# Which engine forms the low parts of the weights, and a planner whose clocks know that DVE and POOL share a way into SBUF

## The chip, the cores and the metric

The kernel runs on one NeuronCore of a Trainium2 chip. The core has five engines with instruction queues of their own: PE (matrix multiplications), DVE (vector operations), ACT (functions and casts), POOL (vector operations on the GpSimd cores) and SP, which here only issues DMAs. Each engine works through its queue in order and waits at its head for what the instruction there needs. Time is device microseconds (us) of one execution. The number compared is the median of several runs.

## The reference

Two blocks follow each other on 256 tokens of width 1024, all in float32. The first block is one layer of a hybrid mixer (two attentions, a gated linear attention, a recurrent unit) and a mixture of 32 experts. The second block has two layers, and each layer is

```python
for i in range(2):
    f = swiglu(rmsnorm(h, ffn1_pre_g[i]), ffn1_w_gate[i], ffn1_w_up[i], ffn1_w_down[i])
    h = h + 0.5 * rmsnorm(f, ffn1_post_g[i])
    m = mixer(rmsnorm(h, mix_pre_g[i]), ...)      # SSD branch + S5 branch, gated, then w_out
    h = h + rmsnorm(m, mix_post_g[i])
    f = swiglu(rmsnorm(h, ffn2_pre_g[i]), ffn2_w_gate[i], ffn2_w_up[i], ffn2_w_down[i])
    h = h + 0.5 * rmsnorm(f, ffn2_post_g[i])
```

`swiglu` is `(silu(x @ w_gate) * (x @ w_up)) @ w_down` with a hidden width of 2816. The mixer multiplies by `w_in`, runs a state space model in chunks (SSD) on one branch and a diagonal complex recurrence (S5) on the other, and multiplies by `w_branch_a`, `w_glu`, `w_branch_b` and `w_out`.

## The kernel before

A product of two float32 matrices is made of three products of a shorter format, fp32r: each operand is split into a high part (the value rounded to fp32r) and a low part (the value less its high part), and PE forms high by high, high by low and low by high (`mm3`). All weights of the dense layers are split on the chip.

**How weights flow.** A unit of weights is 128x2048 floats, 1 MB. SP loads units one after the other into a ring of raw buffers (tiles named `..._raw`). Each unit has two halves of 128x1024. For each half, ACT casts the raw half to the high part (`split_high`, L368, tiles `..._whi`), and then DVE or POOL subtracts the high part from the raw half (`split_low`, L376, tiles `..._wlo`). The subtraction is called "a low" below. `low` (L359) chooses its engine. When both lows of a unit are formed, its raw buffer is free (`drop`) and SP may load the next unit into it. High and low parts live in rings of four halves in the second block, three raw buffers feed them, and PE spends 24 matmuls of 128x256 on each half.

**What sets the order.** The kernel is written out by a planner that runs when the program is built. Every instruction goes through `Engine` (L131), which keeps a clock for each engine: an instruction starts at the latest of its engine's clock and the times at which its operands are written or free, and it ends after a cost by formula (`on_vector`, `on_gpsimd` and so on). The clocks are those of an estimate; on the chip only the order on each queue is left of them. In the stages with `static = False` (the first mixer and the whole second block) the clocks decide three things. `pump` (L339) decides when a high part or a low is put in a queue. `low` decides which engine gets a low: before the change POOL has it if it ends there in time for PE (0.5 us before PE is due at that half, 2.57 us of PE for each half in front of it) or if POOL would end before DVE, and DVE has it otherwise. `either` (L552) chooses DVE or POOL for some other vector operations by their clocks, and `stir` (L466) lets the side work ("threads": the activations of a feed-forward layer, the SSD and S5 branches, the building of the S5 matrices) issue its next step when their clocks are not too far ahead of PE's. During the mixture of experts the order is fixed (`static`), and there `low` isn't asked in this way.

**The stages** of the profiled run, by their borders in us: first mixer with routing 0 to 278, experts 278 to 1255, and then, for each of the two layers of the second block, feed-forward 1, mixer, feed-forward 2: 1255 to 1512, 1512 to 1965, 1965 to 2206, 2206 to 2408, 2408 to 2859, 2859 to 3067. While the first and the third of these six run, `s5_build` (L1007) loads the tables of the S5 matrices of the mixer to come with many small DMAs (tiles `s5b_p`) and multiplies them on whichever engine `either` names.

Names in rows: the part before the first underscore is the stage or thread that made the tile (`ffn`, `bnd` for the boundary between layers, `u`, `z`, `x`, `g`, `glu`, `bb`, `ba`, `wo` for products of the mixer, `ssd`, `dt`, `s5i`, `s5o`, `s5b` for its side work, `k` for what lasts). Since every operation is recorded by `Engine`, all rows have one line, L155.

Of the kernel before, what the change touches and what calls it, by code (L numbers as in the profile page):

```python
# [29 lines left out]
class FM:  # L30


    def __init__(self, tiles):
        self.tiles = tiles
# [8 lines left out]
class Clocks:  # L43
# [4 lines left out]
    def __init__(self, nc):  # L48
        self.nc, self.times, self.base = nc, {}, {}
        self.dma = self.queue = self.end = 0.0  # L50
        self.count, self.table = 0, None
        self.vector, self.gpsimd = Engine(nc.vector, self.on_vector, self), Engine(nc.gpsimd, self.on_gpsimd, self)
        self.scalar, self.tensor, self.sync = Engine(nc.scalar, self.on_scalar, self), Engine(nc.tensor, self.on_tensor, self), Engine(nc.sync, None, self)

    def __getattr__(self, name):
        return getattr(self.nc, name)
# [49 lines left out]
    def busy(self, name):  # L106
        return max([max(t[:2]) for t in self.times.get(name, {}).values()], default=0.0)

    def on_vector(self, name, out, args, kw):
        n = max(a.free_size() for a in (out, *args) if isinstance(a, bass.AP))  # L110
        return 0.07 + 0.06 * any(isinstance(a, bass.AP) and a.free_size() == 1 for a in args) + n * (0.0063 if name == "reciprocal" else 0.00052 if name in self.SINGLE else 0.00104)
# [19 lines left out]
class Engine:  # L131
# [3 lines left out]
    def __getattr__(self, name):  # L135
        f, c = getattr(self.engine, name), self.clocks

        def call(out, *args, **kw):
            w = [out] + [kw[k] for k in ("accum_out",) if k in kw]
            r = [a for a in (*args, *kw.values()) if isinstance(a, bass.AP) and a is not kw.get("accum_out")]  # L140
            start = max([self.clock] + [c.written(a, self) for a in r] + [c.touched(a, self) for a in w])
            if name == "dma_start":
                self.clock = start + (1.0 if self is c.gpsimd else 0.1)
                c.queue = max(c.queue, start) + 0.45
                c.dma = max(c.dma, c.queue + 1.1) + self.spread(out, r)
                end = c.dma + 1.9
            else:
                end = self.clock = start + self.cost(name, out, args, kw)
            for a in w:
                c.mark(a, end, self)  # L150
            for a in r:
                c.mark(a, end)
            c.end = max(c.end, end)
            c.count += 1
            return f(out, *args, **kw)  # L155
        return call
# [22 lines left out]
class Core:  # L179
# [179 lines left out]
    def low(self, h):  # L359

        if self.static:
            return self.q if h % 4 == 3 and self.keys[self.order[h // 2]][0] in self.LENT else self.v
        c = self.nc
        hi = c.written(self.halves[h][0])
        pool = max(self.q.clock, hi) + 2.3
        return self.q if pool <= max(c.tensor.clock + (h - self.uh) * 2.57 - self.LEAN, max(self.v.clock, hi) + 1.14) else self.v

    def split_high(self):  # L368
        u, i = self.order[self.sh // 2], self.sh % 2
# [1262 lines left out]
class Kernel(Block2):  # L1632
# [590 lines left out]
    def mixer1(self, x):  # L2223
# [68 lines left out]
        for j, (n, _) in enumerate(self.WIN):  # L2292
# [9 lines left out]
            if n == "cqk":  # L2302
                def low():
                    nc.scalar.copy(gl, gps)
                    self.give(ps=1)
                self.defer(low)
# [690 lines left out]
```

## Time and profile before

| | |
|---|---|
| median of 3 runs | 3071.73 us (3071.64 to 3073.94) |
| profiled execution | 3076.65 us, its span 3074.4 us |
| PE busy | 2668.1 us, 87% |
| DVE busy | 1689.6 us, 55% |
| POOL busy | 1442.4 us, 47% |
| ACT busy | 1020.0 us, 33% |
| mean granted TensorE clock | 0.950 |

"Busy" of DVE and POOL counts an instruction from its start to its end as recorded, with any time in which it stood still inside it. [...] A "chain" is the work that ended last, followed back from the last instruction.

### The profile page before, as it was taken

To read this page: it belongs to the slowest core of one execution; us is meant where nothing else is said; L and a number is where in the kernel's file an instruction comes from. 1 tells how busy PE (TensorE), PEld (TensorE's weight loads), DVE (VectorE), ACT (ScalarE), POOL (GpSimd) and SP (SyncE) were. 2 spreads that over 40 slices of the span, in tenths; PEclk is the share of its full clock that TensorE was granted. 3 is DMA by queue.
4 is the path that set the end of the run, shared out by engine and by line. 5 is a ranking of instruction groups with operands and counts; after the bars stand their busy time and mean duration, and the time that the engine had idled before them with its cause. 6 is when DMAs were issued, how large, how long until landed. Compare 5 with 4: busy or idle time off the path is not lost.

```text
span 3074.4 us, 55096 instructions
## 1 busy us (share of the span) xinstructions
PE 2668.1 (87%) x22727; PEld 2062.3 (67%) x22727; DVE 1689.6 (55%) x2657; ACT 1020.0 (33%) x1516; POOL 1442.4 (47%) x733
## 2 busy tenths in 40 slices
PE   5768988889889888877989888977999889998998
PEld 4655333333333333577979888977999889888998
DVE  8995242333433211355577888655554685886644
ACT  4562100001000000233445554433444445544444
POOL 7651000000000000256756666756788657766786
PEclk9778999999999999998999999988999999999999
DMA  7526999999999999655545434455555445444453
GB/s 285 191 86 262 420 420 394 420 420 417 418 419 417 414 421 420 255 171 185 195 144 168 157 138 140 162 171 185 192 181 190 157 122 179 151 151 138 162 185 120
DMA packets 146540, 755.09 MB, mean 246 GB/s; under 512 B 47264, under 2 KB 51824, under 8 KB 59760
## 3 DMA queue, kind: packets, MB, share of 16 engines
q1 hardware_dynamic: 140672, 729.30, 62.6%
q0 software_dynamic: 5472, 21.71, 1.9%
q8 instruction: 183, 3.00, 0.4%
q14 instruction: 69, 0.57, 0.1%
q10 hardware_dynamic: 144, 0.52, 0.0%
HBM read 736.50 MB, written 14.97 MB: 244 GB/s over the span
## 4 chain that ended last, share of the span: by engine, by line
PE 36%; DVE 10%; issue 4%; DMA 3%; ACT 2%; POOL 2%; SPq 1%; ACTq 0%; DVEq 0%; POOLq 0%
PE ffn_ps L155 18%; PE x_ps L155 3%; PE ba_ps L155 3%; DVE ssd_p L155 3%; PE g_ps L155 2%; DMA s5b_p<-s_bt 2%; PE glu_ps L155 2%; PE bnd_ps L155 2%; PE z_ps L155 2%; POOL ffn_wlo L155 2%; PE wo_ps L155 1%; DVE x_p L155 1%; PE ssd_ps L155 1%; DVE u_p L155 1%; SPq L155 1%
## 5 line engine op out<-in xcount | busy, mean ns | idle before, releaser
L155 POOL TENSOR_TENSOR ffn_wlo<-ffn_raw,ffn_whi 128x1024 fp32r<-128x1024 f32 x227 | 569.9, 2537 | 178.4 <-ACT ffn_whi L155 172.7
L155 PE MATMUL ffn_ps<-bnd_p,ffn_whi 128*128 128x256 f32 x2560 | 469.2, 285 | 28.8 <-ACT ffn_whi L155 28.8
L155 PEld LDWEIGHTS ffn_ps<-bnd_p,ffn_whi 128*128 128x128 f32 x2560 | 404.5, 194 | 29.6 <-ACT ffn_whi L155 29.6
L155 PE MATMUL ffn_ps<-bnd_p,ffn_wlo 128*128 128x256 f32 x1280 | 366.4, 286 | 13.7 <-POOL ffn_wlo L155 13.7
L155 ACT CAST ffn_whi<-ffn_raw 128x1024 fp32r<-128x1024 f32 x232 | 240.3, 1046 | 259.4 <-PE ffn_ps L155 174.0
L155 PE MATMUL down_ps<-up_place,tr_p 128*32 128x512 f32 (+1 forms) x2048 | 244.0, 614 | 82.1 <-DMA up_place<-edn 82.1
L155 DVE TENSOR_TENSOR ffn_p<-ffn_p,ffn_p 128x256 f32<-128x256 f32 (+1 forms) x184 | 260.9, 1420 | 91.8 <-ACT ffn_p L155 91.4
L155 PE MATMUL ffn_ps<-ffn_p,ffn_whi 128*128 128x256 f32 x1408 | 258.9, 286 | 29.5 <-ACT ffn_whi L155 28.1
L155 PEld LDWEIGHTS ffn_ps<-bnd_p,ffn_wlo 128*128 128x128 f32 x1280 | 248.8, 194 | 15.9 <-POOL ffn_wlo L155 15.9
L155 PE MATMUL up_ps<-down_place,prep_p 128*32 128x512 f32 (+1 forms) x1920 | 224.8, 596 | 21.4 <-DMA down_place<-eup 21.3
L155 PEld LDWEIGHTS ffn_ps<-ffn_p,ffn_whi 128*128 128x128 f32 x1408 | 222.5, 194 | 30.1 <-ACT ffn_whi L155 28.5
L155 PE MATMUL up_ps<-up_place,prep_p 128*32 128x512 f32 (+1 forms) x2048 | 230.2, 595 | 8.3 <-DMA up_place<-eup 8.2
L155 PEld LDWEIGHTS down_ps<-up_place,tr_p 128*32 128x32 f32 x2048 | 67.8, 112 | 244.6 <-issue 200.5
L155 DVE TENSOR_SCALAR glu_p<-up_ps 128x512 f32<-128x512 f32 x64 | 44.1, 691 | 311.7 <-PE up_ps L155 311.7
L155 PE MATMUL ffn_ps<-ffn_p,ffn_wlo 128*128 128x256 f32 x704 | 201.0, 286 | 0.9 <-DVE ffn_wlo L155 0.9
L155 DVE TENSOR_TENSOR ffn_p<-ffn_ps,ffn_p 128x512 f32<-128x512 f32 x80 | 55.1, 689 | 208.6 <-PE ffn_ps L155 208.4
L155 PEld LDWEIGHTS up_ps<-up_place,prep_p 128*32 128x32 f32 x2048 | 61.8, 109 | 150.3 <-issue 129.1
L155 DVE COPY scat_p<-down_ps 128x512 f32<-128x512 f32 x16 | 11.1, 691 | 245.7 <-PE down_ps L155 245.7
L155 PEld LDWEIGHTS up_ps<-down_place,prep_p 128*32 128x32 f32 x1920 | 57.3, 109 | 129.2 <-issue 125.5
L155 PEld LDWEIGHTS ffn_ps<-ffn_p,ffn_wlo 128*128 128x128 f32 x704 | 136.7, 194 | 1.5 <-DVE ffn_wlo L155 1.5
L155 POOL DMA_DIRECT2D ed<-s5b_raw x4 | 2.1, 538 | 262.8 <-DVE s5b_raw L155 262.8
L155 POOL TENSOR_TENSOR scat_wlo<-scat_raw,scat_whi 128x1024 fp32r<-128x1024 f32 x2 | 4.7, 2364 | 251.1 <-ACT scat_whi L155 251.1
(832 smaller groups left out, 6547.7 us busy)
## 6 DMA issues: line engine op xcount, KB each, us to landing
up_place<-eup SPq DMA_DIRECT2D x128, 1024.0 KB, 10.9
up_place<-edn SPq DMA_DIRECT2D x128, 1024.0 KB, 13.7
down_place<-eup SPq DMA_DIRECT2D x120, 1024.0 KB, 14.1
ffn_raw<-gu SPq DMA_DIRECT2D x75, 1024.0 KB, 5.0
ffn_raw<-dn SPq DMA_DIRECT2D x40, 1024.0 KB, 4.9
x_raw<-win SPq DMA_DIRECT2D x22, 1024.0 KB, 5.0
z_raw<-win SPq DMA_DIRECT2D x16, 1024.0 KB, 4.9
g_raw<-win SPq DMA_DIRECT2D x10, 1024.0 KB, 5.4
```

Source lines behind the costliest of these rows:

```text
L155: return f(out, *args, **kw)
```

## The change

`low` turns its preference round: DVE gets a low if it ends there in time for PE, or if DVE would end before POOL; POOL gets it otherwise. The clocks get a function `shared`, which is asked for each instruction of DVE and POOL other than DMAs: it moves the start of the one behind the end of an instruction of the other that runs at that moment. A DVE instruction with an input in PSUM (where matmul results stand) is left out of it. The start so found goes into the clocks, and so into all that the planner decides by them.

```diff
+        self.port = {}
...
+    def shared(self, engine, start, time, ins):
+
+        other = self.port.get(self.gpsimd if engine is self.vector else self.vector, ())
+        if engine is self.vector and any(a.space == bass.MemoryType.PSUM for a in ins):
+            return start
+        for a, b in other:
+            if a <= start < b:
+                start = b
+        mine = self.port.setdefault(engine, [])
+        mine.append((start, start + time))
+        del mine[:-24]
+        return start
...
-                end = self.clock = start + self.cost(name, out, args, kw)
+                time = self.cost(name, out, args, kw)
+                if self is c.vector or self is c.gpsimd:
+                    start = c.shared(self, start, time, r)
+                end = self.clock = start + time
...
-        pool = max(self.q.clock, hi) + 2.3
-        return self.q if pool <= max(c.tensor.clock + (h - self.uh) * 2.57 - self.LEAN, max(self.v.clock, hi) + 1.14) else self.v
+        pool, vec = max(self.q.clock, hi) + 2.3, max(self.v.clock, hi) + 1.14
+        return self.v if vec <= max(c.tensor.clock + (h - self.uh) * 2.57 - self.LEAN, pool) else self.q
```

Of the 520 lows in the program 35 stood on DVE and 485 on POOL before; now 478 stand on DVE and 42 on POOL. DVE's queue grows from 2264 to 2644 rows, POOL's shrinks from 729 to 341. PE's queue has the same 15644 rows and SP's the same 1299.

DVE's queue in the first feed-forward of the second layer (2206 to 2408 us), before; `ffn_p` are the steps of the activation between the two products:

```order
L155 TENSOR_TENSOR ffn_p_2572_18664<-ffn_ps_18577,ffn_p_2549_18567 128x512
L155 TENSOR_TENSOR ffn_p_2573_18665<-ffn_p_2573_18665,ffn_p_2572_18664 128x256
L155 TENSOR_TENSOR ffn_p_2576_18679<-ffn_p_2573_18665,ffn_p_2575_18678 128x256
L155 TENSOR_TENSOR ffn_p_2581_18731<-ffn_ps_18654,ffn_p_2549_18567 128x512
L155 TENSOR_TENSOR ffn_p_2582_18732<-ffn_p_2582_18732,ffn_p_2581_18731 128x256
L155 TENSOR_TENSOR ffn_p_2585_18746<-ffn_p_2582_18732,ffn_p_2584_18745 128x256
```

The same place on DVE now:

```order
L172 TENSOR_TENSOR ffn_p_2581_18741<-ffn_ps_18657,ffn_p_2549_18577 128x512
L172 TENSOR_TENSOR ffn_wlo_18733<-ffn_raw_18556,ffn_whi_18732 128x1024
L172 TENSOR_TENSOR ffn_p_2582_18742<-ffn_p_2582_18742,ffn_p_2581_18741 128x256
L172 TENSOR_TENSOR ffn_p_2585_18768<-ffn_p_2582_18742,ffn_p_2584_18767 128x256
L172 TENSOR_TENSOR ffn_wlo_18771<-ffn_raw_18610,ffn_whi_18770 128x1024
L172 TENSOR_TENSOR ffn_wlo_18801<-ffn_raw_18610,ffn_whi_18800 128x1024
L172 TENSOR_TENSOR ffn_wlo_18831<-ffn_raw_18695,ffn_whi_18830 128x1024
L172 TENSOR_TENSOR ffn_p_2597_18868<-ffn_ps_18799,ffn_p_2549_18577 128x512
```

The lows that POOL had there are on DVE, between the steps of the activation: three lows to each three steps.

In the mixer of the second layer, DVE before, at the `dt` steps on which the SSD branch waits, with steps of the S5 branch between them:

```order
L155 RECIPROCAL dt_p_2909_21084<-dt_p_2909_21084 32x256
L155 SCALAR_TENSOR_TENSOR s5b_p_2305_16810<-s5i_p_2935_21324,s5b_p_2305_16810 128x512
L155 TENSOR_TENSOR dt_p_2908_21083<-dt_p_2908_21083,dt_p_2909_21084 32x256
L155 TENSOR_TENSOR dt_p_2910_21085<-dt_p_2910_21085,dt_p_2908_21083 32x256
L155 SCALAR_TENSOR_TENSOR dt_p_2911_21086<-dt_p_2907_21082,dt_p_2910_21085 32x256
```

And now:

```order
L172 RECIPROCAL dt_p_2908_21091<-dt_p_2908_21091 32x256
L172 SCALAR_TENSOR_TENSOR s5b_p_2304_16817<-s5i_p_2932_21291,s5b_p_2304_16817 128x512
L172 TENSOR_TENSOR z_wlo_21318<-z_raw_21126,z_whi_21317 128x1024
L172 TENSOR_TENSOR z_wlo_21348<-z_raw_21126,z_whi_21347 128x1024
L172 TENSOR_TENSOR dt_p_2907_21090<-dt_p_2907_21090,dt_p_2908_21091 32x256
L172 TENSOR_TENSOR dt_p_2909_21092<-dt_p_2909_21092,dt_p_2907_21090 32x256
L172 SCALAR_TENSOR_TENSOR dt_p_2910_21093<-dt_p_2906_21089,dt_p_2909_21092 32x256
```

Two lows of the `z` weights stand in front of the `dt` steps.

POOL's queue in the second feed-forward of the first layer (1965 to 2206 us) now, after the last addition of the boundary (`k_h`):

```order
L172 TENSOR_TENSOR k_h_65<-k_h_65,bnd_p_2202_16146 128x256
L172 TENSOR_TENSOR s5b_p_2305_16818<-s5b_p_2259_16487,s5b_p_2261_16489 128x1024
L172 TENSOR_TENSOR s5b_p_2306_16819<-s5b_p_2260_16488,s5b_p_2262_16490 128x1024
L172 TENSOR_TENSOR s5b_p_2304_16817<-s5b_p_2305_16818,s5b_p_2306_16819 128x1024
L172 TENSOR_TENSOR s5b_p_2305_16818<-s5b_p_2259_16487,s5b_p_2262_16490 128x1024
```

The same products of the S5 tables stood on DVE before; all 24 of them (12 in each layer) have moved to POOL, and behind the boundary no low of this feed-forward is left there.

## Rows read from the trace of the kernel before

**Rows 1.** Windows by stage: busy us of each engine (instructions), granted clock, DMA.

```profile
0.00:278.00 278.00, 178.29 (x1237) 156.45 (x1241) 239.70 (x421) 133.95 (x270) 155.00 (x124) 0.83 0.51 189
...
1255.00:1512.00 257.00, 211.42 (x1670) 202.67 (x1663) 129.56 (x109) 95.47 (x131) 163.09 (x69) 0.91 0.55 189
1512.00:1965.00 453.00, 405.54 (x3700) 391.82 (x3699) 344.65 (x481) 217.11 (x296) 303.09 (x143) 0.95 0.45 151
1965.00:2206.00 241.00, 204.19 (x1630) 201.04 (x1629) 133.18 (x115) 92.72 (x129) 164.81 (x73) 0.92 0.53 183
2206.00:2408.00 202.00, 199.38 (x1651) 198.26 (x1650) 104.14 (x105) 95.39 (x132) 168.11 (x75) 1.00 0.50 172
2408.00:2859.00 451.00, 404.65 (x3670) 390.48 (x3669) 342.10 (x479) 215.96 (x294) 299.60 (x141) 0.94 0.45 151
```

**Rows 2.** Timeline in a feed-forward layer: start, duration, engine, instruction [idle before].

```profile
1499.84 2.40 POOL L155 TENSOR_TENSOR ffn_wlo<-ffn_raw,ffn_whi 128x1024 fp32r<-128x1024 f32 x1 [0.47 <-ACT ffn_whi L155]
...
1500.12 2.41 DVE L155 TENSOR_TENSOR ffn_p<-ffn_p,ffn_p 128x256 f32<-128x256 f32 x1 [0.64 <-ACT ffn_p L155]
...
1503.00 0.43 DVE L155 TENSOR_TENSOR ffn_p<-ffn_p,ffn_p 128x256 fp32r<-128x256 f32 x1 [0.47 <-ACT ffn_p L155]
...
1503.99 7.53 POOL L155 TENSOR_TENSOR ffn_wlo<-ffn_raw,ffn_whi 128x1024 fp32r<-128x1024 f32 x3 [1.75 <-ACT ffn_whi L155]
```

**Rows 3.** Forms on DVE, second mixer: operation, shapes, count, busy us, mean ns, idle.

```profile
L155 DVE TENSOR_SCALAR ssd_p<-ssd_p,dt_tok 128x128 f32<-128x128 f32 x64 | 30.9, 551 | 0.0
L155 DVE SCALAR_TENSOR_TENSOR x_p<-x_p,k_vecs,ssd_p 128x256 f32<-128x256 f32 x16 | 18.1, 1164 | 0.1
...
L155 DVE TENSOR_TENSOR s5b_p<-s5i_p 128x256 f32<-128x256 f32 x16 | 15.0, 939 | 0.5
L155 DVE SCALAR_TENSOR_TENSOR bb_p<-g_p,bb_p 128x256 fp32r<-128x256 f32 x8 | 14.2, 1778 | 3.9 <-ACT bb_p L155 3.9
...
L155 DVE TENSOR_TENSOR ssd_p<-x_p,ssd_p 128x512 fp32r<-128x512 f32 x8 | 13.8, 1741 | 5.8 <-ACT ssd_p L155 5.7
```

**Rows 4.** Forms on DVE over the whole span.

```profile
L155 DVE TENSOR_TENSOR ffn_p<-ffn_ps,ffn_p 128x512 f32<-128x512 f32 x80 | 55.1, 689 | 208.6 <-PE ffn_ps L155 208.4
...
L155 DVE TENSOR_SCALAR prep_p<-k_iota,route_pos 128x128 f32<-128x128 f32 x32 | 9.0, 280 | 0.0
...
L155 DVE TENSOR_TENSOR ffn_wlo<-ffn_raw,ffn_whi 128x1024 fp32r<-128x1024 f32 x5 | 8.7, 1748 | 77.1 <-ACT ffn_whi L155 77.0
```

**Rows 5.** Forms on POOL over the whole span.

```profile
L155 POOL TENSOR_TENSOR ffn_wlo<-ffn_raw,ffn_whi 128x1024 fp32r<-128x1024 f32 x227 | 569.9, 2537 | 178.4 <-ACT ffn_whi L155 172.7 <-issue 5.2
```

**Rows 6.** Timeline of DVE at the start of the second block.

```profile
1291.27 1.23 DVE L155 TENSOR_TENSOR ffn_wlo<-scat_raw,ffn_whi 128x1024 fp32r<-128x1024 f32 x1 [5.74 <-ACT ffn_whi L155]
```

**Rows 7.** Window in the second mixer, columns as in rows 1.

```profile
2600.00:2790.00 190.00, 167.66 (x1330) 160.20 (x1329) 156.67 (x232) 94.60 (x128) 123.76 (x55) 0.92 0.41 143
```

**Rows 8.** Waits of PE in the second mixer: us in total, times, longest.

```profile
PE ssd_ps L155 <- DVE ssd_p L155: 12.7, 6, 5.1
PE dt_ps L155 <- DVE dt_p L155: 7.8, 2, 4.2
...
PE u_ps L155 <- DVE u_p L155: 4.7, 1, 4.7
```

**Rows 9.** Waits of PE in the feed-forward from 1965 to 2206.

```profile
PE ffn_ps L155 <- ACT ffn_whi L155: 28.8, 3, 13.7
PE ffn_ps L155 <- POOL ffn_wlo L155: 6.8, 5, 1.9
```

**Rows 10.** The chain there, longest pieces: start, us, what.

```profile
1993.90 1.56 POOL ffn_wlo L155
...
2014.23 15.91 DMA s5b_p<-s_bt
...
2139.79 2.40 POOL ffn_wlo L155
```

**Rows 11.** Forms on DVE from 1965 to 2206.

```profile
L155 DVE TENSOR_TENSOR s5b_p<-s5b_p,s5b_p 128x1024 f32<-128x1024 f32 x12 | 27.5, 2314 | 0.2
```

## Prediction

> **What bounds the kernel now.** I read the windows by stage first [rows 1], because the change acts only where the planner works by its clocks. The experts' stage between 278 and 1255 us has a fixed order and stays as it is. In the stages around it the reader is to compare PE's busy time with the stage's length. The feed-forward from 2206 to 2408 is busy for 199.4 of 202 us at full clock: PE is the bound and nothing can be gained. The same work takes 257 us (1255 to 1512) and 241 us (1965 to 2206) where the S5 tables are built beside it, with PE idle for 45.6 and 36.8 us. The mixers take 453 and 451 us with PE idle for 47.5 and 46.4 us, and their clock of 0.95 and 0.94 says that about a tenth of the time ran at the lower level. The first mixer (0 to 278) has DVE busy for 239.7 us.
>
> Then I looked at what makes DVE so busy, in the timeline [rows 2]. An addition-like operation of 128x256 on DVE takes 2.41 us when it starts 0.28 us behind the start of a low on POOL that takes 2.40 us, and 0.43 us when POOL stands still. It ends 0.29 us behind POOL's end: it stood still until POOL was done. Operations with an input in PSUM keep their time: 80 of 128x512 average 689 ns [rows 4].
>
> [...]
>
> **The change part by part.** *A low itself.* On POOL it averages 2.537 us (227 of them, rows 5). On DVE it takes 1.23 us where nothing holds it [rows 6] and 1.748 on average of five [rows 4]. 443 lows move, so POOL loses 443 x 2.54 = 1124 us and DVE gains 443 x 1.23 = 545 us. None of this is on PE's path as such.
>
> *What DVE gets back.* In the second mixer five forms [rows 3] take 30.9 + 18.1 + 15.0 + 14.2 + 13.8 = 92.0 us. Alone they would take 64 x 0.280 + 16 x 0.43 + 16 x 0.43 + 8 x 0.43 + 8 x 0.689 = 40.6 us, with 0.280 and 0.689 from rows 4 and 0.43 from rows 2 (the nearest rows). So 51.4 us or 56% is standing still. Of DVE's 342 us that is 15% if only these five forms are held, 56% if all are. I take 35%, since some of the rest read PSUM.
>
> *A mixer.* I price it in the stretch in which DVE is fullest, 2600 to 2790 [rows 7]: 190 us with DVE busy for 156.7, POOL for 123.8, PE idle for 22.3 and a clock of 0.92. DVE's own work is 156.7 x 0.65 = 102 us. Some 47 of POOL's 55 instructions are lows, and they cost DVE 47 x 1.23 = 58. The planner also gives POOL some SSD products that DVE had (26 more in both mixers by the order); I take 8 us of DVE for 13 of POOL in this stretch. DVE then has 102 + 58 - 8 = 152 us, before any standing still: hardly less than 156.7. What falls is the sum of both engines, which exclude each other for the most part: 102 + 124 = 226 before, 152 + 20 = 172 after if POOL keeps a few lows and those products. So DVE isn't relieved, but what it now does in the same time is the lows too, and PE's waits on it can shrink. The stretch can give at most PE's 22.3 us idle and what the half clock took (0.92 is 16% of 190 us at half, so 15 us). I take a third, 12 us, and 4 us more from the other waits on DVE in the mixer, the `dt` and `u` steps with 7.8 + 4.7 us [rows 8]: 16 us for a mixer. The bounds are +15 us, if DVE becomes the bound there (below), and -60 us, if PE's 46.4 us idle and half of the clock's loss of 27 us (12% of 451 at half) come back whole. Two mixers: -32 us.
>
> *A feed-forward beside the S5 tables.* PE waits 28.8 us in three pieces for high parts and 6.8 for lows [rows 9]. The first come from the burst of small DMAs in SP's queue, 15.9 us of it on the chain [rows 10], and the change leaves the burst in the queue. But after each burst PE runs from one fresh low to the next: lows on POOL have ten pieces of 1.5 us and more on this chain, the first and last with 1.56 and 2.40 us [rows 10], some 25 us together. With 1.23 for 2.54 half of that, 12 us, can go. Raw buffers come free 1.3 us sooner as well, so SP starts each of three late loads sooner: 4 us. Against it stand the 12 products of the tables, on DVE now with 2.314 us each [rows 11] and moved to POOL, which hold a low on DVE for up to 2.4 us each. I take 11 us, between 0 and 25. Both: -22 us.
>
> *The other feed-forwards* are PE's: 0 to -3 us each; with the boundaries, where one or two operations on the way are held for 2 us, I take -4 us in all.
>
> *The first mixer.* By the order seven lows move from POOL to DVE and ten products of the modulation from DVE to POOL, so the time in which one engine excludes the other stays within 4 us (3 x 1.3). I take 0, between -10 and +10.
>
> *New waits.* A low on DVE waits at the head of its queue for ACT's high part, and ACT for PE to free the ring. Behind it wait the activation steps in a feed-forward (three to each three lows) and the SSD and S5 steps in a mixer. Five lows on DVE already did this before, with DVE idle for 77.1 us before them [rows 4]; POOL was idle for 178.4 us before its 227 [rows 5], where nobody waited behind it. In the full feed-forward DVE has 104 us busy of 202 [rows 1], so this is covered; in the mixers it is the first rival.
>
> The sum: -32 - 22 - 4 + 0 = -58 us. The profiled execution took 3076.65 us (2.25 outside its span of 3074.4), so 3018.6 for one like it. That execution lay 4.9 us over the median of 3071.73, so the median comes to 3013.7; I say 3013.
>
> **The rivals.**
>
> *DVE becomes the bound of the mixers, and the kernel gets slower.* For it: DVE's load in the fullest stretch hardly falls (152 of 190 us before any standing still, and with POOL's remaining 20 us nearer to 165), and a low that waits for its high part now stops the SSD chain behind it. Against it: before, the two engines together had 226 us of work in 190. It decides where DVE is busy for over 90% of such a stretch. Price: each stretch 15 us longer, twice, the feed-forwards beside the tables without gain, so +30 - 4, some 3098 at worst, 3085 as a middle. Chance 0.11.
>
> *The waits were the DMA bursts' and PE's anyway.* Only lows on the chain get shorter: a third of the sum, -20 us, 3052. For it: rows 9 and 10 name DMAs. Chance 0.22, and 0.05 more for no change that shows.
>
> *The pair of engines was the bound of all stages in which it works, not only of a third of PE's waits.* Then the mixers give 45 us each and the feed-forwards 20 each: -90 - 40 - 4 = -134, 2938. For it: 226 us of work in 190, and a planner whose clocks now fit the chip and so puts PE's SSD products where their inputs are ready. Against it: the chain through SSD is long by itself. Chance 0.17 for under 2975.
>
> **How the numbers follow.** The forecast, 2975 to 3040, has 0.45; slower 0.11, no change 0.05, the small gain 0.22 (3040 to 3065), the large one 0.17. The measurement tells 0.2%, 6 us, from no change. Faster: 0.45 + 0.22 + 0.17 = 0.84; same 0.05; slower 0.11. The range for 8 of 10 leaves out 0.06 of the large gain and 0.14 above: 2940 to 3062. The forecast's own range is 2975 to 3040.
>
> **What would show it.** Lows of 1.2 to 1.5 us on DVE; the forms of rows 3 shorter by half; POOL's busy time under 550 us; a stage from 2206 to 2408 still of 200 us; mixers of some 435 us and feed-forwards beside the tables of some 246 and 230. The forecast is wrong if a mixer keeps its 451 us with DVE busy for over 90% of 2600 to 2790, if DVE shows long idle times before lows with PE waiting for `ssd` steps behind them, or if the forms of rows 3 keep their times though POOL is idle.

## The result, and the profile after

The changed kernel takes 2990.24 us (median of 4, 2986.40 to 2993.05) where the kernel before took 3072.74 on the same chip (median of 4): a ratio of 0.9731, 95% interval 0.9714 to 0.9747. It is faster by 82.5 us; the prediction said 58 (3013), with 2975 to 3040 as the forecast's range. The profiled execution took 2988.21 us, its span is 2986.5.

A stage begins with its first matmul: that into `route_ps` ends the first mixer, and each later stage begins with one into `bnd_ps`. The experts stand between route and the second block. These borders are not quite those ahead of the prediction (there the second block begins at 1255 us, here at 1278.9), so the columns stand for themselves. In us:

| stage | before | after | difference | predicted |
|---|---|---|---|---|
| start to route | 254.4 | 270.2 | +15.8 | 0 |
| route and experts | 1024.5 | 1026.5 | +2.0 | 0 |
| feed-forward beside S5 tables, layer 0 | 237.8 | 219.6 | -18.2 | -11 |
| mixer, layer 0 | 449.1 | 414.1 | -35.0 | -16 |
| feed-forward beside S5 tables, layer 1 | 243.4 | 227.1 | -16.3 | -11 |
| feed-forward after it | 201.0 | 201.0 | 0 | -4 with the boundaries |
| mixer, layer 1 | 450.7 | 415.2 | -35.5 | -16 |
| last feed-forward and end | 213.5 | 212.8 | -0.7 | (in the -4) |
| sum | 3074.4 | 2986.5 | -87.9 | -58 |

The windows of the changed kernel, one for each of its five stages from the second block on, answer to [rows 1] (columns as there):

```profile
1296.70:1516.30 219.60, 198.93 (x1586) 197.06 (x1586) 128.51 (x150) 93.02 (x129) 36.54 (x17) 0.95 0.56 197
1516.30:1930.30 414.00, 388.59 (x3671) 377.56 (x3672) 335.96 (x552) 217.92 (x293) 92.23 (x68) 0.98 0.49 164
1930.30:2157.40 227.10, 204.69 (x1643) 201.74 (x1641) 136.98 (x167) 94.54 (x131) 42.88 (x22) 0.95 0.55 194
2157.40:2358.40 201.00, 198.34 (x1640) 197.23 (x1640) 127.01 (x168) 96.31 (x132) 12.18 (x11) 1.00 0.50 173
2358.40:2773.60 415.20, 390.01 (x3672) 378.94 (x3673) 336.22 (x552) 218.46 (x293) 92.20 (x68) 0.98 0.50 164
```

In the second mixer GpSimd (POOL) falls from 301 to 92 us, while VectorE (DVE) is busy for 336 us where it was 341, though it now makes the low parts too. Where that room comes from stands in the forms of VectorE in the second mixer, the five of [rows 3] again:

```profile
L172 DVE TENSOR_SCALAR ssd_p<-ssd_p,dt_tok 128x128 f32<-128x128 f32 x64 | 19.3, 366 | 0.0
...
L172 DVE TENSOR_TENSOR s5b_p<-s5i_p 128x256 f32<-128x256 f32 x16 | 8.9, 553 | 0.4
...
L172 DVE SCALAR_TENSOR_TENSOR x_p<-x_p,k_vecs,ssd_p 128x256 f32<-128x256 f32 x16 | 7.2, 479 | 0.1
...
L172 DVE TENSOR_TENSOR ssd_p<-x_p,ssd_p 128x512 fp32r<-128x512 f32 x8 | 6.1, 770 | 2.4 <-ACT ssd_p L172 2.2
...
L172 DVE SCALAR_TENSOR_TENSOR bb_p<-g_p,bb_p 128x256 fp32r<-128x256 f32 x8 | 3.3, 419 | 0.5 <-ACT bb_p L172 0.5
```

Together 44.8 us where they were 92.0. The low parts of the feed-forwards, over the whole span (before: [rows 4, 5]):

```profile
L172 DVE TENSOR_TENSOR ffn_wlo<-ffn_raw,ffn_whi 128x1024 fp32r<-128x1024 f32 x232 | 297.5, 1285 | 200.8 <-ACT ffn_whi L172 200.7
```

What PE waits for in the second mixer. Before, beside the three lines of [rows 8]:

```profile
PE ssd_ps L155 <- DVE x_p L155: 6.3, 1, 6.3
...
PE glu_ps L155 <- DVE glu_wlo L155: 1.8, 1, 1.8
...
PE x_ps L155 <- POOL g_wlo L155: 1.7, 1, 1.7
PE g_ps L155 <- POOL z_wlo L155: 1.4, 1, 1.4
```

The last three are all of PE's waits for low parts, 4.9 us of the 45.6 that PE is idle there, while other steps of VectorE (`ssd_p`, `dt_p`, `x_p`, `u_p`) stand for 31.5. So PE hardly waited for low parts themselves. After, the waits for `u`, `dt` and `x_p` are all but gone, that for the SSD products is not:

```profile
PE ssd_ps L172 <- DVE ssd_p L172: 13.1, 5, 4.3
PE ssd_ps L172 <- POOL ssd_p L172: 7.3, 1, 7.3
...
PE dt_ps L172 <- DVE dt_p L172: 0.7, 1, 0.7
```

And in the second feed-forward beside the tables, against [rows 9]:

```profile
PE ffn_ps L172 <- ACT ffn_whi L172: 17.3, 2, 9.3
PE ffn_ps L172 <- DVE ffn_wlo L172: 4.2, 5, 1.4
```

The second mixer in three pieces tells how PE gained. The borders lie at the same matmuls in both kernels (1,767, then 1,330, then 578). Before:

```profile
2410.20:2600.10 189.90, 166.63 (x1767) 160.26 (x1768) 144.54 (x205) 89.10 (x124) 120.87 (x63) 0.94 0.48 153
2600.10:2790.10 190.00, 167.66 (x1330) 160.14 (x1329) 156.77 (x232) 94.60 (x128) 123.76 (x55) 0.92 0.41 143
2790.10:2860.90 70.80, 70.80 (x578) 70.69 (x577) 39.35 (x40) 31.14 (x39) 56.10 (x23) 0.98 0.49 167
```

After:

```profile
2358.40:2524.40 166.00, 161.21 (x1767) 156.19 (x1768) 146.29 (x225) 84.88 (x117) 44.37 (x35) 1.00 0.55 174
2524.40:2703.00 178.60, 158.20 (x1331) 152.34 (x1330) 145.18 (x265) 102.41 (x137) 47.83 (x33) 0.95 0.45 153
2703.00:2773.60 70.60, 70.60 (x578) 70.42 (x578) 44.75 (x62) 31.17 (x39) 0.00 (x0) 0.98 0.50 167
```

Length less PE's busy time is PE's idle time: 23.3 us fell to 4.8 in the first piece, 22.3 to 20.4 in the second. The same matmuls also take less: 166.6 became 161.2 and 167.7 became 158.2, since the granted clock is 1.00 and 0.95 where it was 0.94 and 0.92. Such a number is a mean: in windows of 2 us from 2410 to 2790 the kernel before has 1.00, 0.50 or values between them. Around PE's one wait for `u` of 4.7 us [rows 8], which ends at 2449.6:

```profile
2442.00:2449.50 7.50, 1.77 (x14) 1.28 (x12) 7.50 (x13) 3.45 (x7) 4.66 (x2) 0.94 0.61 210
2449.50:2455.00 5.50, 5.37 (x26) 4.55 (x27) 2.96 (x8) 1.53 (x3) 2.90 (x2) 0.50 0.30 116
2455.00:2484.00 29.00, 28.79 (x324) 27.79 (x323) 15.05 (x20) 17.15 (x21) 17.63 (x8) 0.99 0.60 182
```

For 5.5 us behind this wait the clock is 0.50. Of the mixer's 35.5 us, 20.4 are idle time and 15.1 are busy time, which goes with the clock.

### The profile page after: what moved, and what is told of

Read it like the earlier page. It is cut to its first block, busy times and chain, and to the rows that moved or that the text cites. A ratio compares the mean times of both kernels' runs of the same rounds, so it can differ in the third digit from the quotient of the medians.

```text
span 2986.5 us, 54948 instructions
## 1 busy us (share of the span) xinstructions
PE 2639.9 (88%) x22727; PEld 2039.1 (68%) x22727; DVE 1722.9 (58%) x3018; ACT 1040.6 (35%) x1536; POOL 478.1 (16%) x362
## 4 chain that ended last, share of the span: by engine, by line
PE 41%; DVE 8%; DMA 4%; ACT 2%; issue 1%; SPq 1%; POOL 0%; ACTq 0%; DVEq 0%
PE ffn_ps L172 19%; PE x_ps L172 3%; PE ba_ps L172 3%; PE glu_ps L172 3%; PE g_ps L172 3%; PE bnd_ps L172 2%; PE z_ps L172 2%; PE wo_ps L172 2%; PE bb_ps L172 2%; DMA s5b_p<-s_bt 1%; PE ssd_ps L172 1%; DVE bnd_p L172 1%; DVE ffn_wlo L172 1%; SPq L172 1%; DVE ssd_p L172 1%
## 5 line engine op out<-in xcount | busy, mean ns | idle before, releaser
L172 PEld LDWEIGHTS ffn_ps<-bnd_p,ffn_whi 128*128 128x128 f32 x2560 | 403.7, 194 | 18.2 <-ACT ffn_whi L172 18.2
L172 DVE TENSOR_TENSOR ffn_wlo<-ffn_raw,ffn_whi 128x1024 fp32r<-128x1024 f32 x232 | 297.5, 1285 | 200.8 <-ACT ffn_whi L172 200.7
L172 PE MATMUL ffn_ps<-ffn_p,ffn_whi 128*128 128x256 f32 x1408 | 259.1, 286 | 16.3 <-ACT ffn_whi L172 16.3
L172 PE MATMUL up_ps<-up_place,prep_p 128*32 128x512 f32 (+1 forms) x2048 | 232.9, 598 | 11.8 <-DMA up_place<-eup 11.6
L172 PE MATMUL up_ps<-down_place,prep_p 128*32 128x512 f32 (+1 forms) x1920 | 224.8, 596 | 17.6 <-DMA down_place<-eup 17.6
L172 DVE TENSOR_TENSOR ffn_p<-ffn_p,ffn_p 128x256 f32<-128x256 f32 (+1 forms) x184 | 89.9, 492 | 43.6 <-ACT ffn_p L172 43.3
L172 ACT COPY prep_p<-prep_ps 128x512 f32<-128x512 f32 x16 | 9.4, 585 | 290.2 <-PE prep_ps L172 290.2
L172 ACT COPY tr_p<-tr_ps 128x512 f32<-128x512 f32 x32 | 18.7, 585 | 220.3 <-PE tr_ps L172 220.3
L172 ACT ACTIVATE glu_p<-glu_p 128x512 f32<-128x512 f32 (+1 forms) x48 | 26.8, 558 | 193.7 <-DVE glu_p L172 193.7
## 6 DMA issues: line engine op xcount, KB each, us to landing
down_place<-eup SPq DMA_DIRECT2D x120, 1024.0 KB, 14.6
```

## The experiments

The theory ("port"): GpSimd's low parts stopped VectorE, and the gain is that they no longer do. The rival ("clocks"): the gain is that the planner's clocks are now true and order the side work better. A third question is the first mixer, which got slower. The weights have 518 low parts (not 520): 35 on VectorE and 483 on GpSimd before, 478 and 40 after. The expectations of the first two runs count 593, because 75 such rows of other tiles, all on VectorE, were counted in.

The stages up to the second mixer, in us, as in the table above (FF: feed-forward; tables: beside the S5 tables), with the span of the profiled execution and the ratio of the medians to the kernel before (e8, e11 and e12 ran once and stand below):

| run | route | experts | FF tables 0 | mixer 0 | FF tables 1 | mixer 1 | span | ratio (95%) |
|---|---|---|---|---|---|---|---|---|
| before | 254.4 | 1024.5 | 237.8 | 449.1 | 243.4 | 450.7 | 3074.4 | |
| after | 270.2 | 1026.5 | 219.6 | 414.1 | 227.1 | 415.2 | 2986.5 | 0.9731 (0.9714 to 0.9747) |
| e1 rule alone | 271.3 | 1020.2 | 222.4 | 411.4 | 227.2 | 411.5 | 2977.7 | 0.9719 (0.9701 to 0.9738) |
| e2 clocks alone | 263.5 | 1023.6 | 224.8 | 437.0 | 228.9 | 436.2 | 3028.4 | 0.9855 (0.9837 to 0.9874) |
| e3 first mixer old | 253.7 | 1025.7 | 224.3 | 416.5 | 228.9 | 416.4 | 2979.2 | 0.9687 (0.9669 to 0.9705) |
| e4 modulation on VectorE | 261.4 | 1026.0 | 221.4 | 416.4 | 227.1 | 416.8 | 2982.8 | 0.9720 (0.9698 to 0.9742) |
| e5 rule after first mixer | 254.0 | 1024.3 | 221.3 | 412.6 | 229.6 | 412.4 | 2967.9 | 0.9664 (0.9648 to 0.9680) |
| e6 clocks, old placement | 272.3 | 1030.2 | 231.2 | 452.6 | 231.8 | 454.4 | 3093.1 | 1.0045 (1.0027 to 1.0063) |
| e7 second subtraction | 268.9 | 1025.3 | 304.0 | 564.0 | 312.5 | 563.9 | 3577.7 | 1.1651 (1.1631 to 1.1670) |
| e9 all low parts on VectorE | 254.0 | 1025.8 | 222.2 | 414.5 | 229.5 | 410.6 | 2970.2 | 0.9656 (0.9640 to 0.9672) |
| e10 MEMSETs on GpSimd | 268.3 | 1026.4 | 247.3 | 426.3 | 255.5 | 426.1 | 3063.5 | 0.9973 (0.9961 to 0.9985) |

**e1, the rule without the clocks.**

```diff
-                if self is c.vector or self is c.gpsimd:
+                if False:
                     start = c.shared(self, start, time, r)
```

> The new rule for the low parts alone; the clocks let VectorE and GpSimd overlap as before. VectorE gets 558 of the 593 low parts (553 with the whole change). Theory 'port' (the gain is that VectorE no longer stands still beside GpSimd's low parts): nearly the whole gain stays, mixers of 412 to 422 us, feed-forwards beside the S5 tables 218 to 230, total 2985 to 3005. Rival 'clocks' (the gain is that the planner's clocks are true, so that TensorE's side work is ordered in time): the mixers stay over 430 and the total at 3030 or more. Theory 'first mixer loses by the rule': route still at 266 to 275 us.

2985.74 us. The whole gain is there without the clocks, as "port" had it, and so is the first mixer's loss.

**e2, the clocks without the rule** (`low` as before).

> The exclusive clocks alone; the old rule for the low parts, so GpSimd keeps 437 of the 593. Theory 'port': VectorE still stands still some 120 us in each mixer, mixers 440 to 455, total 3050 to 3080. Rival 'clocks': most of the gain without the rule, total 2990 to 3030. First mixer: if its loss of 16 us comes from the clocks, route comes at 266 to 275 us here, otherwise at about 254.

3029.48 us: half of the gain, with 46 low parts moved to VectorE by the old rule under the new clocks. That is 20 us below what "port" expected and, by half a microsecond, inside the range of the rival; the mixers (437.0 and 436.2) lie below "port" too, and route, at 263.5, lies between the two values named. So this run alone speaks for the rival as much as for "port". The two halves of the change don't add up (87 and 43 us apart, 82 together), so e6 asks what the clocks gained by.

**e6, the clocks with each low part where it was before** (a list of 518 engines read out of the kernel before).

```diff
-        (v or self.low(self.sl)).tensor_sub(lo, ...)
+        (self.v if LOWS[self.sl] == "V" else self.q).tensor_sub(lo, ...)
```

> The exclusive clocks, with each of the 518 low parts on the engine that it has in the kernel before (a fixed list: 35 on VectorE, 483 on GpSimd). The run with the clocks alone gained 43 us with 437 rows of low parts on GpSimd. Theory 'true clocks gain by the order in which TensorE's side work, the evictions and the tables are written': the gain stays, mixers 435 to 441, total 3024 to 3040. Rival 'they gain by the 46 low parts that moved to VectorE where GpSimd was behind': without that move the mixers are 446 or more, total 3058 to 3075.

3087.82 us, slower than before by 0.45%. The clocks by themselves gain nothing over the whole kernel: e2 lies 58 us below e6 by the 46 low parts that could move and the order that follows from it. The rival "clocks" falls for the mixers and for the sum; the time (above 3075) was outside what either side expected.

Single stages do change, though. The first mixer is 17.9 us longer than before, but the feed-forwards beside the tables are 6.6 and 11.6 us shorter. In the second of these PE waits less for high and low parts, against [rows 9]:

```profile
PE ffn_ps L177 <- ACT ffn_whi L177: 23.6, 2, 12.8
PE ffn_ps L177 <- POOL ffn_wlo L177: 2.0, 1, 2.0
```

GpSimd's 56 `ffn` low parts there still take 2.58 us each. So in these two stages a part of the gain can also be had by order alone.

**e7, the port put under load again.** GpSimd repeats each of VectorE's low parts in the second block (457 of them) into a spare tile; the clocks don't know.

```diff
+        if e is self.v and self.spare is not None:
+            self.q.engine.tensor_sub(self.spare, src[:, 0:1024], hi[:, 0:1024].bitcast(F32))
```

> The changed kernel; for every low part that VectorE makes in the second block, GpSimd makes the same subtraction once more into a tile that nobody reads, and the clocks are not told. Low parts still come from VectorE. Theory 'port': VectorE stands still beside them again, so its instructions beside GpSimd's have means twice their shortest, and with its own low parts on top the mixers take 455 us or more, total 3070 to 3200. Rival 'the gain is that a low part takes 1.23 us on VectorE where it took 2.5 on GpSimd, and what a busy GpSimd costs VectorE is little': mixers under 425, total 2985 to 3005.

3579.50 us, 589 above the changed kernel (1.29 us for each repeated subtraction), far beyond what "port" expected, and on its side. The forms of VectorE from 1300 us on:

```profile
L172 DVE TENSOR_TENSOR ffn_wlo<-ffn_raw,ffn_whi 128x1024 fp32r<-128x1024 f32 x232 | 619.3, 2694 | 57.7 <-ACT ffn_whi L172 57.6
```

A low part on VectorE takes 2694 ns where it took 1285, and PE's waits from 1300 us on name it:

```profile
PE ffn_ps L172 <- DVE ffn_wlo L172: 174.6, 96, 5.1
PE ssd_ps L172 <- DVE ssd_p L172: 58.6, 12, 7.7
```

In the changed kernel these two were 7.8 and 26.4 us.

**e10, the same with a GpSimd that reads next to nothing:** one column is subtracted, so that it starts where the other did, then two MEMSETs.

```diff
+            self.q.engine.tensor_sub(self.spare[:, :1], src[:, :1], hi[:, :1].bitcast(F32))
+            for _ in range(2):
+                self.q.engine.memset(self.spare, 1.0)
```

> As the run with a second subtraction on GpSimd beside each low part, but in its place GpSimd makes a subtraction of one column (so that it starts where the other did) and two MEMSETs of 128x1024 (1.9 us by the stages of the two engines alone, against 2.4). Theory 'what stops VectorE is GpSimd's two-source reading of SBUF, not a busy or late GpSimd': in the second block VectorE's subtractions keep 0.43 us, TENSOR_SCALAR of SBUF rise towards 0.5, total 2985 to 3030. Rival 'GpSimd is late for its own SSD products, or holds the buffers too long': total over 3200.

3062.92 us, between the two expectations. Forms from 1297 us on:

```profile
L401 POOL MEMSET scat_spare<- 128x1024 f32 x912 | 871.0, 955 | 53.2
...
L172 DVE TENSOR_TENSOR ffn_wlo<-ffn_raw,ffn_whi 128x1024 fp32r<-128x1024 f32 x232 | 297.4, 1286 | 248.0 <-ACT ffn_whi L172 247.9
```

VectorE's low parts take the 1286 ns of the changed kernel, so a busy GpSimd doesn't stop them: of e7's 589 us, 517 (3579.5 - 3062.9) go with what GpSimd read. The other 73 are not taken apart by this run. A late GpSimd is one part of them; another can be that TENSOR_SCALAR, one of the forms of [rows 3], has a mean of 544 ns in the second mixer here, where the changed kernel has 366 (e8 shows it held beside MEMSETs alone). PE's waits from 1300 us on:

```profile
PE ffn_ps L172 <- ACT ffn_whi L172: 79.7, 10, 20.3
PE ssd_ps L172 <- DVE ssd_p L172: 31.4, 10, 4.4
PE ssd_ps L172 <- POOL ssd_p L172: 24.7, 8, 7.9
```

The first was 34.1 and the third 14.6 in the changed kernel. The raw buffers stay held until GpSimd has read its column behind its MEMSETs, so the loads and the high parts come later. Before the change GpSimd's low parts held them too.

**e8, the engines alone:** none of the model is computed. Each stage runs one kind of instruction on each engine.

> None of the model is computed: stages in which VectorE, GpSimd and ScalarE run one kind of instruction each, alone or side by side. Theory 'port': a 128x256 subtraction of two SBUF tiles takes 0.43 us alone on VectorE and a mean of over 1 us beside GpSimd's 128x1024 subtractions, some of 2.3 to 2.5; one with a PSUM source stays at 0.45; a TENSOR_SCALAR of SBUF data (0.28 alone) waits as well. If it is the sources alone that clash, a GpSimd MEMSET costs VectorE nothing; if it is every access, it costs as much. Rival 'the long records come from the waits that the scheduler put there': side by side, without such waits, the means stay under 0.5 us and GpSimd's at 2.4.

The tiles' views, VectorE's instructions (ns: shortest, median, longest; start of the first and the last). First alone, then beside GpSimd's 128x1024 subtractions, COPYs and MEMSETs, and with a source in PSUM beside subtractions; the same for TENSOR_SCALAR:

```profile
L54 DVE TENSOR_TENSOR s1tt_v<-x x24: 424/424/425, 6.3 to 16.9; 128x256 f32<-128x256 f32 x24
...
L54 DVE TENSOR_TENSOR s5ttq_v<-x x24: 424/424/2446, 59.2 to 85.9; 128x256 f32<-128x256 f32 x24
...
L54 DVE TENSOR_TENSOR sAtt_cp_v<-x x24: 424/424/1274, 186.3 to 202.7; 128x256 f32<-128x256 f32 x24
...
L54 DVE TENSOR_TENSOR s8tt_set_v<-x x48: 424/424/426, 135.5 to 157.0; 128x256 f32<-128x256 f32 x48
...
L56 DVE TENSOR_TENSOR s7psq_v<-x,ps x48: 420/421/423, 112.7 to 134.1; 128x256 f32<-128x256 f32 x48
...
L55 DVE TENSOR_SCALAR s2one_v<-x x24: 293/294/295, 18.3 to 25.8; 128x256 f32<-128x256 f32 x24
...
L55 DVE TENSOR_SCALAR s6oneq_v<-x x24: 293/294/2384, 87.2 to 111.4; 128x256 f32<-128x256 f32 x24
...
L55 DVE TENSOR_SCALAR s9one_set_v<-x x48: 293/294/1001, 158.4 to 185.1; 128x256 f32<-128x256 f32 x48
```

The forms of three of these stages:

```profile
L54 DVE TENSOR_TENSOR s5ttq_v<-x 128x256 f32<-128x256 f32 x24 | 26.3, 1098 | 0.8
...
L54 POOL TENSOR_TENSOR s5ttq_q<-x 128x1024 f32<-128x1024 f32 x8 | 19.3, 2415 | 0.6
...
L54 POOL TENSOR_TENSOR s4q_q<-x 128x1024 f32<-128x1024 f32 x8 | 18.7, 2338 | 0.6
...
L54 DVE TENSOR_TENSOR sDtt_act_v<-x 128x256 f32<-128x256 f32 x24 | 10.2, 425 | 0.8
```

Beside 8 subtractions of GpSimd, exactly 8 of VectorE's 24 take 2.44 to 2.45 us: one gets through for each of GpSimd's. The other 16, one ahead of GpSimd's first and 15 behind its last, take 0.42. GpSimd hardly notices (2415 ns against 2338 alone). With a source in PSUM a subtraction takes 421 ns, alone and beside them. ScalarE beside VectorE costs it nothing (425 against 424). The long records thus come without any waits that a scheduler placed, and "port" holds, source by source. Beside GpSimd's MEMSETs all 48 of the same subtractions take 0.42 us.

**e3, the first mixer planned as before; e5, the same without the clocks anywhere; e9, as e5 with every later low part that `low` places on VectorE.**

```diff
     def low(self, h):
+        if self.first:
+            pool = max(self.q.clock, hi) + 2.3
+            return self.q if pool <= max(..., max(self.v.clock, hi) + 1.14) else self.v
...
                 ms = k.mixer1(x)
+                k.first = k.nc.first = False
```

> The whole change, but off until the first mixer has been written (old rule, old clocks there); from the experts on as in the changed kernel. Theory 'the first mixer lost 16 us and nothing after it made up for that': route back at about 254 us, total 2971 to 2978. Rival 'the experts wait for their weights anyway': route earlier, but the second block starts where it did (1297 us), total 2985 to 2992.

2977.68 us: route is back at 253.7 and the second block starts at 1279.5 and not at 1296.8. Its stages take 10 us more in the profiled executions (1699.7 against 1689.7), and 12.6 of the 16 us arrive in the median.

> The new rule for the low parts from the experts on, the old one in the first mixer, and the old clocks throughout. Theory 'the first mixer's loss stands by itself, and the clocks add nothing to the rule': the run with the rule alone took 2706 us from route to the end, and the run with the old first mixer reached route at 254 us, so 2960 us of span and 2958 to 2970 us of time. Rival 'what the first mixer gains is lost to the experts' weights': route at 254, the second block still at 1288 to 1292, total 2975 to 2988.

2969.75 us (2964.44 to 2971.89), the upper end of what was expected. This version beats both kernels: 0.9664 of the kernel before against 0.9731 for the change.

> As the run with the rule from the experts on, but there every low part goes to VectorE, without asking the clocks. Theory 'GpSimd's low parts cost more than they help': the 24 or so that the rule still left on GpSimd in the second block held VectorE some 2.4 us each, mixers 405 to 413 us, total 2955 to 2970. Rival 'the clocks rightly keep some on GpSimd where VectorE is behind': mixers 416 to 425, total 2975 to 2995.

2967.50 us, the same as e5 within the intervals. Whether the 18 low parts that the rule leaves on GpSimd in the second block of e5 go there doesn't matter; neither the theory nor the rival is borne out.

**Why the first mixer got slower: e4, e11, e12.** e4 puts all products of the modulation on VectorE (`if True:` for the planner's choice in `ada_unit`).

> The changed kernel with all 48 products of the first mixer's modulation on VectorE (19 there with the change, 29 on GpSimd). Theory 'the loss of the first mixer is the late products on GpSimd with their totals on ScalarE': no product ends after 225 us, route at 252 to 260 us, total 2972 to 2982. Rival 'VectorE's load is what delays the first mixer': 29 more instructions of 1.2 to 2.2 us on VectorE, route at 275 to 300 us, total 2995 to 3020.

2984.39 us, and route comes at 261.4, between the two. The last product ends at 152 us here, and still 7 us are lost; in e1 the last ended at 216 and 17 were lost; before the change it ended at 227. So late products are not the cause, though the order with them off GpSimd loses less. e11 and e12 touch neither rule nor port in the first mixer: e5 with GpSimd's planned cost there raised from 0.00215 to 0.00226 us per element, and e5 with `EARLY` 0.3 for 0.2.

> The run with the rule from the experts on; in the first mixer the planner takes GpSimd's instructions for 5% longer. Neither rule nor port is touched there. Theory 'the first mixer was tuned to one order, and any other order costs it': route at 260 to 275 us where it was at 254. Rival 'the new rule and the new clocks do harm there of themselves': route at 250 to 257.

> The run with the rule from the experts on; in the first mixer a side step may be written 0.3 us ahead of its inputs, not 0.2. Theory 'tuned to one order': route at 260 to 275 us. Rival 'rule and clocks do harm of themselves': route at 250 to 257.

Route at 265.1 and 263.1 us, where e5 had 254.0; 2983.13 and 2972.47 us (one run each). Two changes that have nothing to do with the port cost 11 and 9 us, while the runs that keep the old order (e3, e5, e9) reach route at 253.7 to 254.0. Rule and clocks cost 9 to 18 (e2, e1, e6), so a part of their loss may be their own. In the profiles of before, after, e1, e2, e4, e6, e11 and e12 the last matmul group of the gated-attention branch (`gla_ps<-gla_p,k_blk`) starts 28 to 30 us ahead of route, at 225.4 us before and at 232 to 243 in the others. Of before and of the change:

```profile
225.37 1.02 PE L155 MATMUL gla_ps<-gla_p,k_blk 128*128 128x256 f32 x4
...
254.42 0.40 PE L155 MATMUL route_ps<-route_sel,k_ones 128*128 128x32 f32 x2 [0.68 <-DVE route_sel L155]
```

```profile
240.72 2.08 PE L172 MATMUL gla_ps<-gla_p,k_blk 128*128 128x256 f32 x4
...
270.25 0.40 PE L172 MATMUL route_ps<-route_sel,k_ones 128*128 128x32 f32 x2 [0.68 <-DVE route_sel L172]
```

The first mixer ends with this branch, and the order that the kernel before had there suits it better, by 7 us or more, than every other order that ran. Which step of the branch is held longest stays open.

## Why the prediction was right, and where not

*The mechanism* was right: VectorE stood still until GpSimd was done [rows 2]. e7, e8 and e10 show it by putting it back, by itself, and with its reading taken out. The signs named ahead are there: low parts of 1.29 us, the forms of [rows 3] at 44.8 us (40.6 was said for them alone), GpSimd busy for 478 us in all, the feed-forward with nothing beside it at 201.

*"I take a third, 12 us, and 4 us more from the other waits"* is the term of the sum that was mis-sized. The stretch for which 12 us stood gave 11.4 (190.0 to 178.6), so its size was right by luck: the 12 us were a third of PE's idle time and the clock's loss together, and it came from busy time (9.5, with the clock) more than from idle time (1.9). PE's idle time fell so little because a wait for SSD products on GpSimd, which has 13 more of these instructions now, grew from 0.6 to 7.3 us; the prediction named the move, but not this wait. One reading behind it was wrong as well: 41 of GpSimd's 55 instructions there are low parts, not 47. The 4 us stood for everything outside it, which gave 23.9 (189.9 to 166.0). There the waits for `u` and `dt` (4.7 + 7.8 us, [rows 8]) went almost whole, not by a third. The wait of `ssd_ps` for `x_p` (6.3 us, one piece) wasn't counted, and went too. With the waits gone the clock stayed at 1.00 for the whole 166 us, worth another 5.4 us on the same 1,767 matmuls. The prediction weighed the clock (the half it counts with is the 0.50 seen behind the wait for `u`) in the fullest stretch and in its bounds, but not behind these short waits. Two mixers: -70.5 us against -32.

*"11 us, between 0 and 25"* for a feed-forward beside the tables was 18.2 and 16.3. In the second one PE's waits for high parts fell from 28.8 us [rows 9] to 17.3, those for low parts from 6.8 to 4.2. The larger part thus lies where the prediction gave 4 us, in the waits for late loads. Whether raw buffers that come free sooner gave it stays open. e10, in which buffers are held longer again, has these stages at 247.3 and 255.5 us, which agrees, but e10 makes GpSimd late for its other work too; and e6 gets 6.6 and 11.6 us there by another order, with no low part moved. (The chain there has eleven pieces of low parts of 1.5 us and more, 27 us, where the prediction read ten and 25.)

*"I take 0, between -10 and +10"* for the first mixer failed: +15.8 us. It priced seven low parts and ten products, so the work that moves, and not the order of the steps around them. e11 and e12 change neither the rule nor `shared` there and cost 11 and 9 us by another order.

*The rivals.* VectorE did not become the bound: it is busy for 336 of 415 us in the mixer. "The waits were the DMA bursts' anyway" gave too little: e1 alone keeps 87 us. The pair of engines as the bound of all stages was the nearest of the rivals in the mixers (-45 said, -35 seen) and in the feed-forwards (-20 said, -17 seen); the support it drew from the planner's truer clocks is refuted by e1, and by e6 for the mixers. The gains of the other stages come to 105.7 us (70.5 + 34.5 + 0.7) where 58 were said, and the loss of the first mixer and the experts (15.8 + 2.0) took part of this error back. That the total lies inside the forecast's range is thus in part luck: e5, without the first mixer's loss, comes to 2969.75 us, below the range.

## What to carry to other kernels

Where VectorE worked on two SBUF sources beside a GpSimd that subtracted two SBUF tiles, their times nearly added up (e8: 2.48 us from one pair to the next, of 0.42 and 2.34 alone). Read the shortest against the mean time of one form on VectorE before giving GpSimd more work, and price the removal of a short wait on PE with the clock behind it (0.50 for 5.5 us behind a wait of 4.7 here). Making the planner's clocks true to the chip gained nothing in sum while the placement was held (e6). A stage that every other order slows, as the first mixer here, should be left out of a change to the planner, or measured by itself: here that was worth 16 us (e1 to e5, 2985.7 to 2969.8).

## What the runs showed of the hardware that was not expected

- In e8 a short VectorE instruction loses against a long one of GpSimd and not the other way: 0.42 us become 2.45 while GpSimd goes from 2.338 to 2.415 us. With equal shapes, 128x1024 on both, both lose: VectorE's shortest is 1.22 us and its median 3.24, and GpSimd's mean rises from 2.34 to 3.21.
- A GpSimd MEMSET, which reads nothing, leaves the two-source subtraction at 424 ns but holds one TENSOR_SCALAR of one SBUF source in three (16 of 48, beside 16 MEMSETs) to 1.00 us, where it takes 0.29 alone.
- GpSimd's COPY and TENSOR_SCALAR of 128x1023 and 128x1024 take 1.10 and 1.05 us, its subtraction of two tiles 2.34. Beside the COPYs VectorE's longest subtraction takes 1.27 us, and its longest TENSOR_SCALAR beside COPYs and TENSOR_SCALARs 1.15 and 1.09, where beside the subtractions the two take 2.45 and 2.38.
